# Bias tables of a two-block transformer: one matmul for a table's heads, and a DMA that repeats its eight rows

## Chip, cores and metric

One NeuronCore of a Trainium2 chip. The metric is device time in microseconds, the median of several executions; all times of this document are of that one core.

## The reference

Two transformer blocks on 512 tokens of width 1024, all in fp32. Every layer is `x + norm(mixer(norm(x)))`, then `x + norm(ffn(norm(x)))`. What the change touches are two bias tables that are added to attention scores:

```python
# block 1, dilated attention: 3 groups of 8 heads, dilations 1, 4, 16, bands of 128
bucket = t5_bucket(np.clip(m, 0, band) * dilation)          # m = i + band - k
bias = jnp.transpose(bias_table[bucket], (2, 0, 1))         # bias_table: 32 buckets x 8 heads
logits = einsum('bxhnqd,bxhnkd->bxhnqk', qs, kk) * scale + bias
logits = jnp.where(mask, logits, NEG_INF)
...
# block 2, differential attention: 4 heads of two maps, rel_bias_2 of 32 buckets x 8
bias = rel_bias[t5_bucket_2(k_pos[None, :] - q_pos[:, None])]
```

The bias depends on the difference of two positions alone, so a head's bias is a Toeplitz matrix: one row of values, shifted by one from each query to the next.

## The kernel before

The order of work is: block 1 (dilated attention, an FFN with a convolution, a linear recurrence, a second such FFN), then block 2 (three mixers side by side, attention over a memory, an FFN with squared ReLU; twice). Activations stand feature-major in SBUF (`hT`) as a high and a low part of reduced fp32, and every weight product is three matmuls: L161 (high, high), L162 (high, low), L163 (low, high), 512 columns each. A block of 128 outputs is 8 × 3 = 24 of them. A weight comes as a raw tile of 512 KB from HBM by SP's queue (L141, three raw buffers); ScalarE casts the high part (L148), VectorE subtracts for the low part (L149); five such pairs can be held. All DMAs of this document are issued by SP, in the order of its instructions, and an instruction that waits holds up those behind it.

The Python code is generators that run side by side; a Tile framework then sets the order of the instructions on each engine from the emission order, priorities and the buffers of the pools. So a step that is emitted earlier, or costs less, can move others.

A bias table is made by `toeplitz` (L275 to 288). `oh` is a constant one-hot matrix of 33 rows (32 buckets and a mask row) by L columns, `tb` the bias table of buckets by heads. For a head the matmul L285 takes `oh` as the moving operand and the head's column of `tb`, repeated to 128 columns, as the stationary one, so that the head's row of L values stands on all 128 output partitions. fp32 matmuls appear as two records each. ScalarE copies them (L286) to a staging tile `fz` of 128 × 1024, and when that is full a DMA (L288) writes it to a DRAM scratch of [128 rows, heads, L]. Reading the scratch with a row pitch one less than a row gives the shifted rows (`toeplitz_view`), for `bias` (L403 to 405, tile `bi`) in block 1 and for `da` (L1057, tile `bd`) in block 2.

There are four tables: tz0 (L = 383), tz1 and tz2 (L = 255) in `setup` of `attn` (L311 to 324), and `da_scr` (L = 639, 32 rows) in `setup2` (L791). The staging tile of tz0 is one of the four buffers of tag "qk"; that of the others is the single buffer of tag "scr", which is also the scratch of the norms' squares (`rms`, L199).

What sets when the tables are made: `START` (L83) is the list of steps before the first products, in which each `t0` is one head of tz0; the rest follow between the first Q and K blocks. `setup2` and what follows it in `prep` (the keys and values of the memory, `mem_kv`, and small columns) are `fill` of the second FFN of block 1: after each block of its up products (`ups`) from the eighth on, one `next(fill)` runs one step; a head of the table is a step.

Of the kernel before, what the change touches and what calls it, by code (L numbers as in the profile page):

```python
# [31 lines left out]
def pipe(gens):  # L32
    """software pipeline: each round starts one generator (None: no new one) and advances the ones under way"""
    live = []
    for g in gens:
        if g is not None:
            live.append(g)
        live = [x for x in live if next(x, 0) is None]
        yield
    while live:  # L40
        live = [x for x in live if next(x, 0) is None]
        yield
# [11 lines left out]
def both(*gens):  # L54
    """generators run side by side, as one; a step that ends with "more" goes on after the others' steps"""
    live = list(gens)
    while live:
        r = [next(g, 0) for g in live]
        while "more" in r:
            r = [next(g, 0) if v == "more" else v for g, v in zip(live, r)]  # L60
        live = [g for g, v in zip(live, r) if v is None]
        yield


def woven(*streams):
    """streams of (generator, steps per round), until all end"""
    live = list(streams)
    while live:
        live = [(g, n) for g, n in live if all([next(g, 0) is None for _ in range(n)])]
        yield  # L70
# [11 lines left out]
# order of the first norms (n: a step of a tile's), weights (w) and heads of the bias table (t)  # L82
START = "n0 t0 t0 t0 n0 n1 n0 w0 w1 n1 n2 n2 n1 n3 n2 n3 n3".split()  # L83
# mixers of the second block: units of attention by tile and head (d: differential, s: stick-breaking pair,
# m: latent pair), the projections emitted beside them (c, v: by tile; l: weights; u: latent up-projection by tile;
# s: stick-breaking by block), and how many output products follow each further round
# [6 lines left out]
class Net:  # L93
# [31 lines left out]
    def bank(self):  # L125
        """accumulator bank"""
        return self.ps.tile([P, 512], F32, tag="acc", name=self.nm("acc"), bufs=6)

    def tbank(self):
        """bank for transposes"""  # L130
        return self.ps.tile([P, 512], F32, tag="tr", name=self.nm("tr"), bufs=2)

# [1 line left out]
    def weight(self, src, shape, pool=None, tag="w", lo=None):  # L134
        """src: HBM view of shape [128, a, b] with a*b <= 1024, split into hi + lo."""
        return self.cut(self.load(src, shape), shape, pool, tag, lo)
# [15 lines left out]
    def w_in(self, W, c0, width=P):  # L152
        """feature-major weight blocks: [128 k, 8 kb, width]"""
        return self.weight(W[:, c0:c0 + width].rearrange("(k p) c -> p k c", p=P), (W.shape[0] // P, width))
# [10 lines left out]
    def split_to(self, dst, src, hi=None):  # L165
        """dst [P, 2, ...] hi/lo of src (fp32 view in SBUF or PSUM)"""
        self.nc.scalar.copy(dst[:, 0], src)  # L167
        self.nc.vector.tensor_sub(dst[:, 1], src, dst[:, 0].bitcast(F32))  # L168

# [6 lines left out]
    def rsqrt(self, ss, scale, shape, tag):  # L176
        """rsqrt(ss * scale + EPS) on a small fp32 tile"""
# [15 lines left out]
    def rms(self, hs, n=D):  # L193
        """1/rms over the free axis of the two halves hs"""
# [10 lines left out]
    def to_T(self, src, dst, t):  # L205
        """src [P tok, 1024] -> dst[:, hi/lo, kb, t*128..]"""
# [9 lines left out]
    def prenorm(self, t, gb, dst=None, src=None, xn=None):  # L216
        """steps: the row's rms, the normalised tile (scaled by ScalarE where VectorE is the busier), its transposes"""
# [16 lines left out]
    def postnorm(self, hs, y, t, gb):  # L234
        """x[t] += rmsnorm(hs) * g, by way of y"""
# [7 lines left out]
    def after(self, t, xn=None):  # L243
        """x[t] is final for this sublayer: start the next sublayer's norm, or store"""
        if self.next_g is None:
            self.nc.sync.dma_start(self.out[t * P:(t + 1) * P], self.x[:, t])
            return
        if self.next_gb is None:
            self.next_gb = self.bcast_row(self.next_g)
        yield from self.prenorm(t, self.next_gb, xn=xn)  # L250

    # feature-major block: psum[128 cols, 512 tok] over all 8 kb
# [7 lines left out]
    def cols(self, srcs, n, pool, name):  # L260
        """each src (n*128 values, contiguous in HBM) -> tile [128, len(srcs), n], value n*128+p at [p, n]"""
# [13 lines left out]
    def toeplitz(self, table, oh, L, heads, scratch, stage, bank=None):  # L275
        """rows F[h, t] = sum_b table[b, h] * oh[b, t], repeated on 128 rows of HBM scratch [128, heads, L]"""
        nc = self.nc
        kb = oh.shape[0]
        per = 1024 // L
        for h0, h1 in halves(heads, per):  # L280
            f = stage()
            for h in range(h0, h1):
                for c0, c1 in halves(L, 512):
                    b = (bank or self.tbank)()
                    nc.tensor.matmul(b[:, :c1 - c0], table(h).to_broadcast([kb, P]), oh[:, c0:c1], start=True, stop=True)  # L285
                    nc.scalar.copy(f[:, (h - h0) * L + c0:(h - h0) * L + c1], b[:, :c1 - c0])  # L286
                yield
            nc.sync.dma_start(scratch[:, h0:h1], f[:, :(h1 - h0) * L].rearrange("p (h t) -> p h t", t=L))  # L288

    def toeplitz_view(self, scratch, L, h0, nh, c0, n):  # L290
        """[128 i, nh, n]: F[h, c0 + kk - i]"""
# [3 lines left out]
    def attn(self, l):  # L295
# [4 lines left out]
        with ExitStack() as cx:  # L300
# [10 lines left out]
            def setup():  # L311
                tb = one.tile([33, 24], F32, name="tb")
                nc.sync.dma_start(tb[:32], a["rel_bias"])
                nc.vector.memset(tb[32:33], NEG)
                for g in range(3):
# [5 lines left out]
                    yield from self.toeplitz(lambda h, g=g: tb[:, g * 8 + h:g * 8 + h + 1], oh, LS[g], 8, scr[g],  # L321
# [52 lines left out]
            def start():  # L374
                """norms of the four tiles and the first values' weights, in the order of their use"""
# [241 lines left out]
    def exp_small(self, out, x, pool, n):  # L617
        """exp on a small [128, n] fp32 tile, x in [-87, 88] after clamping"""
# [20 lines left out]
    def log_sigmoid(self, x, out, pool, n):  # L639
        """out = min(x, 0) - log1p(exp(-|x|)) on a small [128, n] tile"""  # L640
# [18 lines left out]
    def lru_setup(self, one):  # L659
        """per-channel constants of the recurrent mixer"""  # L660
# [117 lines left out]
    def out_proj(self, W, A, yt, gpost, mid):  # L778
        """yt[t] = (8 k-blocks A) @ W, then x += rmsnorm(yt) * gpost; mid(g) emits g, the first half of K, and
        returns a pool for weights of the second one"""  # L780
# [12 lines left out]
    def setup2(self, pool):  # L793
        """bias rows of the differential attention, masks, rope tables"""
# [3 lines left out]
        tb = pool.tile([32, 8], F32, name="tb2")  # L798
        nc.sync.dma_start(tb, a["rel_bias_2"])
        oh = self.nrm.tile([P, D], F32, tag="xn", name=self.nm("oh"))[:32, :L]  # L800
        nc.sync.dma_start(oh, a["c_ohda"])
        yield from self.toeplitz(lambda h: tb[:, h:h + 1], oh, L, 8, self.da_scr,
# [7 lines left out]
    def prep(self, l, pool):  # L810
        """what layer l of the second block needs beside its tokens"""
# [45 lines left out]
    def head_rstd(self, src, nh, dh, tag):  # L857
        """1/rms per head of src [P, nh, dh]"""
# [7 lines left out]
    def proj_tok(self, W, c0, width, consume, early=False):  # L866
        """token-major h @ W[:, c0:c0+width]: one generator per token tile, then consume(t, bank)"""
# [19 lines left out]
    def below(self, x, fill=0.0):  # L887
        """fills a [128, 128] block on and above its diagonal"""
# [3 lines left out]
    def exp_rows(self, p, stat, w):  # L892
        """p = exp(p - max), stat [P, 2]: max in, sum out"""
# [4 lines left out]
    def trans_blocks(self, src, n, pool):  # L898
        """transposes of n 128-column blocks of src [P, n*128] -> tile [P, n*128]"""
# [8 lines left out]
    def o_scaled(self, b, nh, dh, c, pool, tag, bufs):  # L908
        """rmsnorm over each head of b * c (c [P, nh] or None) -> token-major tile"""
# [16 lines left out]
    def y_write(self, on, nb, gcol, kb, i):  # L926
        """transposes on [P tok, nb*128], scales by gcol per feature, hi/lo into hT[:, :, kb:kb+nb, tile i]"""
# [10 lines left out]
    def mem_kv(self, l):  # L938
        """keys and values of the memory, a generator"""
# [33 lines left out]
    def mix(self, l):  # L973
        a, nc = self.a, self.nc
        W, Wo = a["w_in_2"][l], a["w_out_2"][l]
        with ExitStack() as cx:
# [64 lines left out]
            # one attention unit = one head (pair) of one query tile  # L1041
# [244 lines left out]
            def gate(*what):  # L1286
                """until all of what is done"""
# [3 lines left out]
            def settle():  # L1291
                """the layer's input back, and the memory attention's buffers"""
# [28 lines left out]
            def paced(g, ns):  # L1321
                """g, by ns steps per round, then by one"""
# [13 lines left out]
    def memory(self, l, x2, b_qz, b_o, b_n, b_g, ons):  # L1336
        """memory attention of one token tile, in buffers of 1024 columns"""
# [82 lines left out]
    def ff_head(self, l):  # L1420
        """first blocks of ffn2(l) for the tokens of the last two tiles, while the first tile is still on its way"""
# [68 lines left out]
    def down_gen(self, W, ks, A, tail):  # L1490
        """token-major partial product over k-blocks ks; tail(t, half, bank) consumes each."""
# [15 lines left out]
    def down_last(self, W, ks, A, tail, post=None, pool=None):  # L1507
        """as down, one token tile after another, each followed by post(t) and the next sublayer's norm"""
# [131 lines left out]
```

## Time and profile before

| | us |
|---|---|
| three executions | 3063.64, 3059.31, 3063.38 |
| median | 3063.38 |
| the profiled execution, its span | 3061.5 |
| TensorE busy in it | 3012.3 |
| VectorE, ScalarE, GpSimd busy | 1669.2, 1254.2, 170.5 |

The profile is of one execution, taken on the chip. Its span is the time from the first instruction's start to the last one's end. A timeline lists one engine's instructions by start time; in brackets stands how long the engine had been idle before one and what ended that. `out<-in` names the tiles by the program's names, and `x4` is four instructions in a row. Engines are PE (TensorE), DVE (VectorE), ACT (ScalarE), POOL (GpSimd), SP; SPq rows are DMA issues.

### The profile page before, as it was taken

How to read it: one execution, taken by the hardware profiler on the slowest of the kernel's cores; microseconds unless marked ns; L12 is line 12 of the kernel's file. 1: busy time of each engine (PE TensorE's matmuls, PEld its weight loads, DVE VectorE, ACT ScalarE, POOL GpSimd, SP SyncE). 2: the span in 40 equal slices, each digit the busy share in tenths (PEclk: the TensorE clock that was granted, in tenths of full speed). 3: DMA queues.
4: the chain of work that ended last, by engine and by line, in shares of the span. 5: the costliest groups of instructions: out<-in, count | busy, mean ns of one | idle time of the engine just before them, and what ended most of it. 6: DMA issues, size and time to landing. Idle time of an engine off the chain costs nothing.

```text
span 3061.5 us, 37833 instructions
## 1 busy us (share of the span) xinstructions
PE 3012.3 (98%) x14594; PEld 2488.2 (81%) x14594; DVE 1669.2 (55%) x3166; ACT 1254.2 (41%) x2427; POOL 170.5 (6%) x257
## 2 busy tenths in 40 slices
PE   9999999999999999999999999999999999999999
PEld 6889898888888877877787777888887877888887
DVE  3232323364655696644557678754545578754443
ACT  4232322354333575433335467542323457632222
POOL 0000000000000041000001022000000013000000
PEclk9999999999999999999999999999999999999999
DMA  6221222333333323333334332132333333123332
GB/s 185 71 83 56 83 63 76 97 102 92 97 96 91 89 75 112 100 98 107 105 97 138 103 118 84 28 124 84 118 94 111 110 86 104 49 76 91 96 95 70
DMA packets 340023, 287.40 MB, mean 94 GB/s; under 512 B 14041, under 2 KB 280676, under 8 KB 339844
## 3 DMA queue, kind: packets, MB, share of 16 engines
q1 hardware_dynamic: 339844, 284.99, 30.7%
q8 instruction: 115, 1.88, 0.3%
q14 instruction: 64, 0.52, 0.1%
HBM read 272.34 MB, written 12.62 MB: 93 GB/s over the span
## 4 chain that ended last, share of the span: by engine, by line
PE 54%; DVE 6%; ACT 2%; issue 1%; POOL 1%; DMA 1%; POOLq 0%; ACTq 0%; DVEq 0%
PE acc L161 16%; PE acc L163 16%; PE acc L162 16%; PE acc L1048 1%; PE tr L212 1%; PE acc L1061 1%; PE tr L903 1%; DVE w L149 1%; PE acc L1193 1%; PE acc L1387 0%; PE acc L1367 0%; DVE z L1105 0%; DMA raw<-in_w_in_dram 0%; ACT w L148 0%; PE tr L285 0%
## 5 line engine op out<-in xcount | busy, mean ns | idle before, releaser
L149 DVE TENSOR_TENSOR w<-raw,w 128x1024 fp32r<-128x1024 f32 (+1 forms) x456 | 553.9, 1217 | 489.2 <-ACT w L148 488.6
L161 PE MATMUL acc<-hT,w 128*128 128x512 f32 (+1 forms) x1992 | 761.0, 383 | 1.5 <-ACT w L148 1.2
L163 PE MATMUL acc<-hT,w 128*128 128x512 f32 (+1 forms) x1992 | 757.6, 380 | 3.0 <-DVE w L149 2.8
L162 PE MATMUL acc<-hT,w 128*128 128x512 f32 (+1 forms) x1992 | 759.0, 381 | 0.4 <-DVE hT L168 0.4
L148 ACT CAST w<-raw 128x1024 fp32r<-128x1024 f32 (+2 forms) x464 | 477.9, 1033 | 551.5 <-PE acc L163 469.3
L163 PEld LDWEIGHTS acc<-hT,w 128*128 128x128 f32 x1992 | 374.9, 188 | 83.5 <-DVE w L149 4.3
L161 PEld LDWEIGHTS acc<-hT,w 128*128 128x128 f32 x1992 | 374.4, 188 | 82.9 <-issue 2.6
L162 PEld LDWEIGHTS acc<-hT,w 128*128 128x128 f32 x1992 | 374.6, 188 | 78.5 <-DVE hT L168 1.1
L161 PE MATMUL acc<-w,act 128*128 128x512 f32 x896 | 355.1, 397 | 0.8 <-ACT act L167 0.8
L162 PE MATMUL acc<-w,act 128*128 128x512 f32 x896 | 354.3, 396 | 0.0
L163 PE MATMUL acc<-w,act 128*128 128x512 f32 x896 | 352.8, 394 | 0.0
L161 PE MATMUL acc<-w,hT 128*128 128x256 f32 (+2 forms) x896 | 335.1, 374 | 0.8 <-ACT w L148 0.8
L163 PE MATMUL acc<-w,hT 128*128 128x256 f32 (+2 forms) x896 | 326.0, 364 | 0.0
L162 PE MATMUL acc<-w,hT 128*128 128x256 f32 (+2 forms) x896 | 325.1, 363 | 0.0
L562 DVE SCALAR_TENSOR_TENSOR u<-acc,cw,u 128x511 f32<-128x511 f32 x192 | 143.5, 748 | 205.9 <-ACT u L560 202.8
L161 PEld LDWEIGHTS acc<-w,hT 128*128 128x128 f32 x896 | 205.6, 229 | 21.1 <-issue 2.4
L162 PEld LDWEIGHTS acc<-w,hT 128*128 128x128 f32 x896 | 205.8, 230 | 17.1 <-issue 2.4
L163 PEld LDWEIGHTS acc<-w,hT 128*128 128x128 f32 x896 | 205.6, 229 | 15.2
L161 PEld LDWEIGHTS acc<-w,act 128*128 128x128 f32 x896 | 168.3, 188 | 42.6 <-ACT act L167 2.1
L163 PEld LDWEIGHTS acc<-w,act 128*128 128x128 f32 x896 | 168.3, 188 | 41.3 <-DVE act L168 0.6
L162 PEld LDWEIGHTS acc<-w,act 128*128 128x128 f32 x896 | 168.4, 188 | 39.2
L560 ACT ACTIVATE u<-acc,cw 128x512 f32<-128x512 f32 x96 | 74.7, 778 | 219.5 <-PE acc L163 219.3
(376 smaller groups left out, 3307.5 us busy)
## 6 DMA issues: line engine op xcount, KB each, us to landing
raw<-in_w_ff_dram SPq DMA_DIRECT2D x128, 512.0 KB
raw<-in_ffn_w_up_dram SPq DMA_DIRECT2D x96, 512.0 KB
raw<-in_attn_w_qkv_dram SPq DMA_DIRECT2D x72, 512.0 KB
raw<-in_ffn_w_down_dram SPq DMA_DIRECT2D x48, 512.0 KB
raw<-in_w_in_dram SPq DMA_DIRECT2D x40, 512.0 KB
raw<-in_lru_w_in_dram SPq DMA_DIRECT2D x16, 512.0 KB
raw<-in_w_out_dram SPq DMA_DIRECT2D x16, 512.0 KB
x<-in_x_dram SPq DMA_DIRECT2D x8, 512.0 KB
```

Source lines behind the costliest of these rows:

```text
L148: nc.scalar.copy(w[:, 0], raw)
L149: (lo or nc.vector).tensor_sub(w[:, 1], raw, w[:, 0].bitcast(F32))
L161: mm(out, sh, mh, start=first, stop=False)
L162: mm(out, sh, ml, start=False, stop=False)
L163: mm(out, sl, mh, start=False, stop=last)
L212: nc.tensor.transpose(b[:, j * P:(j + 1) * P], src[:, k * P:(k + 1) * P], self.ident)
L560: nc.scalar.activation(u, b, AF.Identity, bias=cw[:, 3, j:j + 1], scale=cw[:, 2, j:j + 1])
L562: nc.vector.scalar_tensor_tensor(u[:, s:], b[:, :S - s], cw[:, i, j:j + 1], u[:, s:], op0=ALU.mult, op1=ALU.add)
L903: nc.tensor.transpose(b[:, j * P:(j + 1) * P], src[:, j * P:(j + 1) * P], self.ident)
L1048: nc.tensor.matmul(o[:, oc:oc + dv], pT[:, k * P:(k + 1) * P], v(k), start=(k == 0), stop=(k == i))
L1061: nc.tensor.matmul(b[:, :w], QZ[:, h, m, i * P:(i + 1) * P], kT[:, h, :w], start=True, stop=True)
L1193: nc.tensor.matmul(b[:, :w], MT[:96, i, 0, h], MT[:96, :i + 1, 1, h], start=True, stop=True)
```

## The change

One matmul makes a whole table: the stationary operand is a slice of 128 columns of `tb`, of which the first eight are the heads of the table, so head h's row stands on output partition h alone (the other partitions hold other columns or zeros and are not copied). One copy takes eight partitions, and one DMA per table reads the eight rows, each 128 times (a step of 0 in the source), and writes the same scratch. `tb` becomes 33 × 144, `tb2` 32 × 128, the added columns zeroed on VectorE. A table is one step of the generator. Nothing that reads the scratch is changed; comments and docstrings were taken out of the file as well, so line numbers move by two to four.

```diff
-START = "n0 t0 t0 t0 n0 n1 n0 w0 w1 n1 n2 n2 n1 n3 n2 n3 n3".split()
+START = "n0 t0 n0 n1 n0 w0 w1 n1 n2 n2 n1 n3 n2 n3 n3".split()
...
     def toeplitz(self, table, oh, L, heads, scratch, stage, bank=None):
         nc = self.nc
-        kb = oh.shape[0]
-        per = 1024 // L
-        for h0, h1 in halves(heads, per):
-            f = stage()
-            for h in range(h0, h1):
-                for c0, c1 in halves(L, 512):
-                    b = (bank or self.tbank)()
-                    nc.tensor.matmul(b[:, :c1 - c0], table(h).to_broadcast([kb, P]), oh[:, c0:c1], start=True, stop=True)
-                    nc.scalar.copy(f[:, (h - h0) * L + c0:(h - h0) * L + c1], b[:, :c1 - c0])
-                yield
-            nc.sync.dma_start(scratch[:, h0:h1], f[:, :(h1 - h0) * L].rearrange("p (h t) -> p h t", t=L))
+        f = stage()
+        for c0, c1 in halves(L, 512):
+            b = (bank or self.tbank)()
+            nc.tensor.matmul(b[:, :c1 - c0], table, oh[:, c0:c1], start=True, stop=True)
+            nc.scalar.copy(f[:heads, c0:c1], b[:heads, :c1 - c0])
+        nc.sync.dma_start(scratch.rearrange("r h t -> h r t"), f[:heads, None, :L].to_broadcast([heads, P, L]))
+        yield
...
             def setup():
-                tb = one.tile([33, 24], F32, name="tb")
-                nc.sync.dma_start(tb[:32], a["rel_bias"])
-                nc.vector.memset(tb[32:33], NEG)
+                tb = one.tile([33, 16 + P], F32, name="tb")
+                nc.vector.memset(tb[:, 24:], 0.0)
+                nc.sync.dma_start(tb[:32, :24], a["rel_bias"])
+                nc.vector.memset(tb[32:33, :24], NEG)
...
-                    yield from self.toeplitz(lambda h, g=g: tb[:, g * 8 + h:g * 8 + h + 1], oh, LS[g], 8, scr[g],
+                    yield from self.toeplitz(tb[:, g * 8:g * 8 + P], oh, LS[g], 8, scr[g],
...
     def setup2(self, pool):
-        tb = pool.tile([32, 8], F32, name="tb2")
-        nc.sync.dma_start(tb, a["rel_bias_2"])
+        tb = pool.tile([32, P], F32, name="tb2")
+        nc.vector.memset(tb[:, 8:], 0.0)
+        nc.sync.dma_start(tb[:, :8], a["rel_bias_2"])
...
-        yield from self.toeplitz(lambda h: tb[:, h:h + 1], oh, L, 8, self.da_scr,
+        yield from self.toeplitz(tb, oh, L, 8, self.da_scr,
```

SP's queue at the start, before (the names are tiles; `tz_132` is tz0's scratch, `raw` a weight, `oh` a one-hot matrix of the 255-column tables):

```order
L288 DMA tz_132<-fz_133 128x766
L288 DMA tz_132<-fz_141 128x766
L141 DMA raw_347<-in_attn_w_qkv_dram 128x8x128
L141 DMA raw_381<-in_attn_w_qkv_dram 128x8x128
L141 DMA raw_417<-in_attn_w_qkv_dram 128x8x128
L317 DMA oh_481<-in_c_oh_dram 33x255
L317 DMA oh_513<-in_c_oh_dram 33x255
L141 DMA raw_451<-in_attn_w_qkv_dram 128x8x128
```

And the same place of SP's queue in the changed kernel, with the semaphores that each row waits for (DMAHW is a DMA's landing; `tz_133`, `tz_283` and `tz_341` are tz0, tz1 and tz2):

```order
L284 DMA tz_133<-fz_134 8x128x383 [waits DMAHW1_49,Activation_49]
L315 DMA oh_281<-in_c_oh_dram 33x255 [waits DMAHW2_49,DVE_49,PE_49]
L315 DMA oh_339<-in_c_oh_dram 33x255 [waits DMAHW3_49,DVE_49,PE_49]
L141 DMA raw_349<-in_attn_w_qkv_dram 128x8x128 [waits DMAHW4_49]
L403 DMA bi_378<-tz_133 128x2x256 [waits DMAHW5_49,DMAHW1_49]
L141 DMA raw_384<-in_attn_w_qkv_dram 128x8x128 [waits DMAHW6_49,Activation_49]
L284 DMA tz_283<-fz_284 8x128x255 [waits DMAHW7_49,Activation_49]
L141 DMA raw_415<-in_attn_w_qkv_dram 128x8x128 [waits DMAHW0_49]
L141 DMA raw_446<-in_attn_w_qkv_dram 128x8x128 [waits DMAHW4_49,DVE_49]
L284 DMA tz_341<-fz_342 8x128x255 [waits DMAHW2_49,Activation_49]
```

The first Q and K weights (raw_347, raw_381 before, raw_349, raw_384 now) moved from the place right behind the first transfers of tz0 to behind the two `oh` loads, the second of them also behind a read of tz0; and tz1 and tz2 moved up between them.

ScalarE at the first Q blocks, before (`q` is the evacuation of a Q block, `w` a weight's cast):

```order
L148 CAST w_419<-raw_417 128x1024 [waits DMAHW5_49]
L148 CAST w_453<-raw_451 128x1024 [waits DMAHW0_49,DVE_49,PE_49]
L370 COPY x<-acc_291 128x512 [waits PE_49]
L286 COPY fz_341<-acc_342 128x383 [waits PE_49]
L148 CAST w_553<-raw_551 128x1024 [waits DMAHW1_49,DVE_49]
L336 ACTIVATE q_236<-acc_346 128x512 [waits PE_49]
L148 CAST w_620<-raw_618 128x1024 [waits DMAHW2_49,DVE_49,Activation_49]
```

And there in the changed kernel:

```order
L368 COPY x<-acc_290 128x512 [waits DVE_49,PE_49]
L283 COPY fz_284<-tr_285 8x255 [waits PE_49,Activation_49]
L148 CAST w_351<-raw_349 128x1024 [waits DMAHW4_49]
L148 CAST w_386<-raw_384 128x1024 [waits DMAHW6_49]
L334 ACTIVATE q_230<-acc_348 128x512 [waits PE_49]
L334 ACTIVATE q_230<-acc_383 128x512 [waits PE_49]
L283 COPY fz_342<-tr_343 8x255 [waits DMAHW7_49,Activation_49]
L148 CAST w_417<-raw_415 128x1024 [waits DMAHW0_49]
```

Before, five weights are cast ahead of the first evacuation; now two are, and the third stands behind the copy of tz2, which waits for the landing of tz1.

ScalarE before the norm of the memory in block 1's second FFN, before:

```order
L286 COPY fz_10501<-tr_10502 128x512
L286 COPY fz_10501<-tr_10505 128x127
L148 CAST w_10692<-raw_10690 128x1024
L167 CAST act_10497<-u_10487 128x512
L199 ACTIVATE sq_10595,ss_10596<-mem_10591 128x512 x2
L199 ACTIVATE sq_10680,ss_10681<-mem_10676 128x512 x2
```

And now, with the waits:

```order
L283 COPY fz_9599<-tr_9600 8x512 [waits PE_49]
L283 COPY fz_9599<-tr_9603 8x127 [waits PE_49]
L167 CAST act_9590<-u_9580 128x512 [waits DVE_49]
L558 ACTIVATE u_9667<-acc_9607,cw 128x512 [waits PE_49]
L148 CAST w_9800<-raw_9798 128x1024 [waits DMAHW1_49]
L566 ACTIVATE u_9667<-u_9667 128x512 [waits DVE_49,Activation_49]
L558 ACTIVATE u_9672<-acc_9608,cw 128x512 [waits PE_49]
L167 CAST act_9677<-u_9667 128x512 [waits DVE_49]
L199 ACTIVATE sq_9693,ss_9694<-mem_9689 128x512 [waits DMAHW5_49,DMAHW2_49,Pool_49]
L199 ACTIVATE sq_9693,ss_9694<-mem_9689 128x512
L148 CAST w_9835<-raw_9833 128x1024 [waits DMAHW3_49]
```

The square (`sq`) stood behind the last of eight copies before and stands behind the only one now; the casts of the next up block (w_9835) stand behind it. On TensorE 144 weight products lie between the table's two matmuls and the transposes of this norm in the changed kernel (over 210 between the last table matmuls and these transposes before). The place of the transposes (`tr_9989<-ident,xn_9692`; `acc_9768` is the last of the down products ahead, `acc_9831` the next up block) is now

```order
L161 MATMUL acc_9768<-w_9800,act_9590 128x512
L162 MATMUL acc_9768<-w_9800,act_9590 128x512
L163 MATMUL acc_9768<-w_9800,act_9590 128x512
L212 MATMUL tr_9989<-ident,xn_9692 128x128
L161 MATMUL acc_9831<-hT,w_9835 128x512
L162 MATMUL acc_9831<-hT,w_9835 128x512
L212 MATMUL tr_9989<-ident,xn_9692 128x128 x3
```

so the next up block comes behind the first of these transposes, which comes behind the norm.

## Rows read from the trace of the kernel before

**Rows 1.** The page's head: the span, and each engine's busy time, share of the span, instructions.

```profile
span 3061.5 us, 37833 instructions
PE 3012.3 (98%) x14594; PEld 2488.2 (81%) x14594; DVE 1669.2 (55%) x3166; ACT 1254.2 (41%) x2427; POOL 170.5 (6%) x257
```

**Rows 2.** TensorE's timeline from the start: start, duration, line, out<-in; what ended idle time.

```profile
3.08 4.17 PE L285 MATMUL acc<-oh,tb 33*128 33x383 f32 x6 [3.08 <-DMA oh<-in_c_oh_dram]
9.04 1.97 PE L212 MATMUL tr<-ident,xn 128*128 128x128 f32 x8 [1.80 <-DVE xn L229]
12.29 1.64 PE L285 MATMUL acc<-oh,tb 33*128 33x383 f32 x2
```

**Rows 3.** TensorE's timeline around one head of table 0, between two Q blocks.

```profile
30.71 0.50 PE L161 MATMUL acc<-hT,w 128*128 128x512 f32 x1
36.17 0.40 PE L163 MATMUL acc<-hT,w 128*128 128x512 f32 x1
36.50 0.91 PE L285 MATMUL acc<-oh,tb 33*128 33x383 f32 x2
37.34 0.50 PE L161 MATMUL acc<-hT,w 128*128 128x512 f32 x1
```

**Rows 4.** TensorE's timeline around two heads of table 1, and the first scores.

```profile
56.08 0.40 PE L163 MATMUL acc<-hT,w 128*128 128x512 f32 x1
56.40 1.12 PE L285 MATMUL tr<-oh,tb 33*128 33x255 f32 x4
57.46 0.50 PE L161 MATMUL acc<-hT,w 128*128 128x512 f32 x1
68.03 3.30 PE L428 MATMUL acc<-k,q 128*128 128x128 f32 x16
```

**Rows 5.** TensorE's timeline around one head of block 2's table.

```profile
1349.56 0.40 PE L163 MATMUL acc<-hT,w 128*128 128x512 f32 x1
1349.89 1.34 PE L285 MATMUL tr<-oh,tb 32*128 32x512 f32 x4
1351.16 0.50 PE L161 MATMUL acc<-hT,w 128*128 128x512 f32 x1
```

**Rows 6.** Line L288, the table DMAs: who waited for them (us, times).

```profile
  ACT fz L286: 5.8, 3
  ACT sq L199: 0.4, 1
```

**Rows 7.** The page's costliest groups: the low and the high part of a weight.

```profile
L149 DVE TENSOR_TENSOR w<-raw,w 128x1024 fp32r<-128x1024 f32 (+1 forms) x456 | 553.9, 1217 | 489.2 <-ACT w L148 488.6
L148 ACT CAST w<-raw 128x1024 fp32r<-128x1024 f32 (+2 forms) x464 | 477.9, 1033 | 551.5 <-PE acc L163 469.3
```

**Rows 8.** The DMA view: the table transfers, their count and KB each.

```profile
da_scr<-fz SPq DMA_DIRECT2D x8, 319.5 KB
tz<-fz SPq DMA_DIRECT2D x4, 510.0 KB
tz<-fz SPq DMA_DIRECT2D x4, 383.0 KB
```

**Rows 9.** Two windows: busy PE, PEld, DVE, ACT, POOL; PEclk, DMA share, GB/s.

```profile
10.00:20.00 10.00, 9.23 (x45) 7.54 (x44) 7.68 (x12) 7.28 (x17) 1.10 (x2) 1.00 0.94 301
1163.00:1173.00 10.00, 7.11 (x19) 5.38 (x20) 9.39 (x12) 5.15 (x7) 0.00 (x0) 0.66 0.43 118
```

**Rows 10.** SP's timeline: the first Q and K weights.

```profile
14.85 2.72 SPq L141 DMA_DIRECT2D raw<-in_attn_w_qkv_dram  x3
```

**Rows 11.** ScalarE's timeline: the first norm's squares.

```profile
5.91 0.63 ACT L199 ACTIVATE sq<-x 128x512 f32<-128x512 f32 x1 [0.71 <-DMA x<-in_x_dram]
```

**Rows 12.** TensorE's timeline after a stall of 2.84 us in a later stage.

```profile
1166.62 0.80 PE L163 MATMUL acc<-hT,w 128*128 128x512 f32 x1 [2.84 <-DVE w L149]
1167.22 0.63 PE L161 MATMUL acc<-hT,w 128*128 128x512 f32 x1
1171.85 0.39 PE L163 MATMUL acc<-hT,w 128*128 128x512 f32 x1
```

## The prediction, made before the changed kernel ran

> **What bounds the kernel now.** I read the page's head first: TensorE is busy 3012.3 of 3061.5 us [rows 1], so some 49 us of the whole span are not its own work, and whatever takes TensorE work away shortens the kernel unless TensorE then waits for something else. Next I read TensorE's timeline around each table. The reader is to see the table matmuls standing in the middle of the stream of weight products, with nothing idle beside them [rows 2 to 5]. Then I read who waits for the table transfers: ScalarE, 5.8 us in three waits for a staging buffer, and 0.4 us before the memory norm [rows 6]. So in the kernel before, the transfers cost nothing on TensorE and the table matmuls cost their full length.
>
> **What is removed, by duration.**
> Table 0 (383 columns). The first three heads take 4.17 us from 3.08, and TensorE stands before its next work until 9.04 anyway [rows 2]: their removal is worth nothing. The fourth costs 1.64 [rows 2]. Heads five to eight each sit between two weight products: from the product before to the product after it is 37.34 − 36.17 = 1.17, and products otherwise follow each other every (36.17 − 30.71) / 23 = 0.24, so one costs 0.93 and four cost 3.7 [rows 3].
> Tables 1 and 2 (255 columns): a pair costs 57.46 − 56.08 − 0.24 = 1.14, so 0.57 a head [rows 4]; 14 of 16 go, 8.0 us. Six of these heads stand behind the first scores (68.03), 3.4 us of the 8.0.
> Block 2 (639 columns): 1351.16 − 1349.56 − 0.24 = 1.36 a head [rows 5]; seven go, 9.5 us.
> Sum of the gain on TensorE: 1.6 + 3.7 + 8.0 + 9.5 = 22.8 us.
> ScalarE loses 35 copies. It waits for others in all these stretches, so this is worth nothing by itself. The two added memsets stand at places where VectorE has no work of the path (the first while the first loads are on their way); at most they are one VectorE operation of the costly kind, 1.22 us [rows 7]; I take 0.
>
> **What is added: the same bytes out of eight partitions.** Before, each table left 128 partitions in transfers of 128 rows: 4 × 383 KB for table 0 (tz0), 2 × 510 KB each for tables 1 and 2 (tz1, tz2), 8 × 319.5 KB for block 2 [rows 8]; at 1024 bytes to a KB that is 1.57, 1.04, 1.04 and 2.62 MB. Now each is one transfer from 8 partitions. No row shows a transfer that reads so few partitions, so I bound its rate. In the busiest stretch the sixteen engines move 301 GB/s at a share of 0.94 [rows 9], 320 at full share. Upper end: the transfer has eight outer rows, so it may use as few as half of the engines, each at its full rate, 160 GB/s. Lower end: the rate goes with partitions, 320 × 8 / 128 = 20 GB/s. The ends are a factor of eight apart and the nearest row (128 partitions, sixteen engines) decides only the upper one, so I take the geometric middle, 57 GB/s, and keep both.
> [...]
>
> **What waits at the start (57 GB/s).** Two things move. On SP's queue the first Q and K weights, issued from 14.85 on right behind the first tables [rows 10], now stand behind the 255-column tables' oh loads, which wait for TensorE's transposes of the last norms; tz1 stands behind a bias load that waits for tz0's landing, and tz2 behind third and fourth weight blocks. On ScalarE the casts that ran two blocks ahead now stand behind the copy into fz, which waits for the table before it. And a weight of 128 rows uses the engines that the table occupies, so it lands when the table has.
> - The queues are at 0.94 until some 12 us with x tiles and weights. tz0: 12 + 1569/57 (27.5) = 39.5. First Q weight behind it; cast 1.03 and low part 1.22 [rows 7] with their semaphores, some 3.5: first Q product at 43 (before: 30.71 [rows 3]). Two blocks of 5.7 end at 54.
> - tz1 is issued about 43, 1044/57 = 18.3 us: 62. Copy, cast, low part: third block at 66; TensorE stands 11 us. Two blocks end at 77.
> - tz2 issued at 66 lands at 85; fifth block at 88.5, another 11 us idle; it ends at 94.5. First scores at 94.5 in place of 68.03 [rows 4]: **+26.5**, the removed work before them already counted.
> - The removed heads behind them: **−3.4**.
>
> **What waits in block 2.** The copy of the table is issued at once, 2617/57 = 46 us. The square of the memory norm (ScalarE, sq) uses the same one buffer as fz. Before, its wait was 0.4 us, since the last small copy was a transfer of 319.5 KB [rows 6, 8]. Now it waits the 46 us, about 1 after the matmul. From sq to the transposes takes 9.04 − 5.91 = 3.1 us in the first norm [rows 2, 11]. So the transposes start 50 us after the table matmul. In the changed order they stand 144 weight products behind it, 144 × 0.24 = 34 us (the shifts of the other fillers move nothing that waits). ScalarE's casts stand behind sq too, so TensorE idles 50 − 34 = **+16**, and the gain there is **−9.5**.
> **The clock.** [...] At the start a loss ahead of a landing is absorbed by it; two remain, the last stall there and that in block 2: **+4.8**.
> Everything later moves unchanged: the small columns and the memory keys come some steps earlier and hide behind products as before, 0.
> **Sum:** 26.5 − 3.4 + 16 − 9.5 + 4.8 = +34.4 on 3061.5. The profiled execution's own span stands 1.9 below the median, so I add to the median: 3063.4 + 34.4 = 3097.8, say **3098**.
>
> **Rivals.**
> *Hidden transfers, faster.* The eight engines run at full rate, 160 GB/s, or the rows are spread over all sixteen, so that the eight partitions are no limit. tz0 lands at 22, tz1 takes 6.5 us and the block-2 table 16, well inside the 34. What is left of the waits: the first, third and fifth Q blocks still find a cast some 2 us late, since the casts lost their lead (6), and the memory norm's transposes wait some 3.5 for a square now close ahead of them. −22.8 + 9.5 = −13.3: 3050. It decides from where the landings stop mattering. At 80 GB/s: tz0 lands at 31.6, first block 35, tz1 48, third block 51.5, tz2 51.5 + 13 = 64.5, fifth 68, scores 74 (+6); −3.4; block 2: 33 + 4 − 34 = 3, −9.5; clock and slips 4: 0. So **above some 80 GB/s it is faster, below slower**. For it: the bytes do not grow and the upper bound comes from a row. Against: no row shows a source of few partitions.
> [...]
> *Near the crossing, the same.* Between 77 and 84 GB/s the two cancel: 3063, a narrow case.
> *Strictly by partition.* 20 GB/s: tz0 78 us, tz1 and tz2 52 each: scores at 12 + 78 + 3.5 + 52 + 3.5 + 52 + 3.5 + 6 = 210 (+142), −3.4; block 2: 131 + 4 − 34 = 101, −9.5; clock 5: +235, 3298.
> *Not the saving it says.* Were TensorE to take eight times as long for the eight-row output, 22.8 us would stay. One matmul has the form of one head before (33 or 32 rows in, 128 columns of stationary), so this is excluded by the rows.
>
> **How the numbers follow.** A measurement of this kernel tells 0.2% (6 us) from no change. Forecast, slower by the table transfers, 0.70; hidden transfers 0.23; the same 0.05; by partition 0.02. The forecast's own range, from 72 GB/s (+11: tz0 is 5.7 shorter, tz1 and tz2 3.8 each, block 2 9.6) to 48 (+55, the same four terms longer by 5.2, 3.5, 3.5 and 8.6), is 3075 to 3119. The range takes in the faster rival and a little below: 3047 to 3120.
>
> **What would show it.** In the changed profile: an empty TensorE of some 11 us before the first, the third and the fifth Q block, each ended by a weight cast whose raw waited behind a table; the first scores at about 94; ScalarE's sq before the memory norm waiting tens of us for da_scr; table transfers of 27, 18, 18 and 46 us. Transfers of 10, 7, 7 and 16 us and first scores near 65 would make the prediction wrong.

## The result, and the profile after

| | us |
|---|---|
| kernel before, median of 4 | 3062.62 |
| changed kernel, median of 4 (3103.58 to 3105.08) | 3104.45 |
| ratio, 95% interval | 1.014 [1.0126, 1.0155] |
| span of the profiled execution, before and after | 3061.5, 3101.8 |

It is slower by some 42 us; 3098 had been predicted. Every kernel of this document was timed with the kernel before run beside it, whose median was 3060.85 to 3062.62. The page's head of the changed kernel (compare [rows 1]):

```profile
span 3101.8 us, 37640 instructions
PE 2989.4 (96%) x14524; PEld 2481.5 (80%) x14524; DVE 1671.6 (54%) x3168; ACT 1242.0 (40%) x2392; POOL 170.5 (5%) x257
```

TensorE has 22.9 us less work (3012.3 to 2989.4), and the span is 40.3 longer, so 63.2 us of idle time were added. Where they lie is read by cutting both spans at the same five events: the first scores, the first product with the values, the last scores, the first matmul of block 2's table, the first scores of block 2. The windows of the kernel before (columns as in [rows 9]):

```profile
0.00:68.03 68.03, 62.39 (x284) 46.52 (x284) 25.78 (x34) 30.83 (x58) 3.01 (x13) 1.00 0.61 184
68.03:212.40 144.37, 143.97 (x687) 126.13 (x686) 43.49 (x131) 43.71 (x107) 0.00 (x0) 1.00 0.29 86
212.40:586.70 374.30, 373.42 (x1882) 336.98 (x1883) 108.12 (x281) 96.94 (x208) 0.00 (x0) 1.00 0.24 71
586.70:1349.50 762.80, 747.51 (x3542) 611.47 (x3541) 479.52 (x677) 354.50 (x532) 59.01 (x58) 0.99 0.32 95
1349.50:1744.20 394.70, 391.89 (x1704) 309.53 (x1704) 225.95 (x344) 155.27 (x242) 18.20 (x20) 1.00 0.36 110
1744.20:3061.50 1317.30, 1293.14 (x6502) 1057.58 (x6500) 786.33 (x1703) 572.98 (x1283) 90.23 (x166) 1.00 0.30 91
```

and of the changed kernel:

```profile
0.00:104.28 104.28, 57.36 (x254) 45.26 (x255) 25.09 (x34) 25.00 (x43) 3.02 (x13) 0.82 0.61 124
104.28:244.40 140.12, 139.76 (x675) 124.24 (x673) 44.65 (x133) 42.81 (x101) 0.00 (x0) 1.00 0.29 86
244.40:618.60 374.20, 373.37 (x1883) 337.09 (x1884) 108.23 (x281) 97.11 (x208) 0.00 (x0) 1.00 0.24 71
618.60:1379.60 761.00, 747.44 (x3544) 611.25 (x3543) 480.31 (x677) 354.90 (x534) 58.19 (x58) 1.00 0.32 96
1379.60:1786.30 406.70, 380.64 (x1673) 306.13 (x1672) 226.98 (x344) 149.46 (x227) 17.96 (x20) 0.97 0.38 105
1786.30:3101.80 1315.50, 1290.85 (x6502) 1057.51 (x6500) 786.39 (x1703) 572.77 (x1283) 91.36 (x166) 1.00 0.29 91
```

First column after the colon: the length. From window to window the change is **+36.3, −4.3, −0.1, −1.8, +12.0, −1.8**, in all +40.3 (the two −1.8 are within the spread of the kernel before, 3059.3 to 3063.6). Two stages lose: the start, and the stage with block 2's table. Who TensorE waited for in the changed kernel (us in total, times, longest):

```profile
PE tr L212 <- DVE xn L229: 32.7, 8, 24.7
PE acc L161 <- ACT w L148: 23.1, 3, 11.4
PE tr L282 <- DMA oh<-in_c_oh_dram: 14.2, 1, 14.2
```

The 24.7 is the wait before the memory norm's transposes; the other two are the start, as TensorE's timeline shows (answers to [rows 3, 4]; the number in brackets is the idle time ahead):

```profile
44.26 2.04 PE L282 MATMUL tr<-oh,tb 33*128 33x255 f32 x4 [14.15 <-DMA oh<-in_c_oh_dram]
46.91 0.80 PE L161 MATMUL acc<-hT,w 128*128 128x512 f32 x1 [0.61 <-ACT w L148]
72.47 0.79 PE L161 MATMUL acc<-hT,w 128*128 128x512 f32 x1 [11.38 <-ACT w L148]
96.96 0.79 PE L161 MATMUL acc<-hT,w 128*128 128x512 f32 x1 [11.06 <-ACT w L148]
```

Now the transfers. SP's timeline, with ScalarE's next to it, gives issue and landing of each table; a landing is read from the first instruction that stood waiting for it (answers to [rows 8, 10]; `...` stands for rows left out):

```profile
5.69 0.37 SPq L284 DMA_DIRECT2D tz<-fz  x1
21.35 4.82 SPq L315 DMA_DIRECT2D oh<-in_c_oh_dram  x2
43.83 0.39 SPq L403 DMA_DIRECT2D bi<-tz  x1
45.92 0.30 SPq L284 DMA_DIRECT2D tz<-fz  x1
...
70.06 0.30 SPq L284 DMA_DIRECT2D tz<-fz  x1
...
93.64 0.36 SPq L403 DMA_DIRECT2D bi<-tz  x1
...
1381.14 0.30 SPq L284 DMA_DIRECT2D da_scr<-fz  x1
```

```profile
69.67 0.36 ACT L283 COPY fz<-tr 8x255 f32<-8x255 f32 x1 [7.94 <-DMA tz<-fz]
71.38 1.04 ACT L148 CAST w<-raw 128x1024 fp32r<-128x1024 f32 x1 [1.34 <-DMA raw<-in_attn_w_qkv_dram]
...
95.87 1.04 ACT L148 CAST w<-raw 128x1024 fp32r<-128x1024 f32 x1 [21.69 <-DMA raw<-in_attn_w_qkv_dram]
...
1435.37 0.63 ACT L199 ACTIVATE sq<-mem 128x512 f32<-128x512 f32 x1 [40.20 <-DMA da_scr<-fz]
```

tz0 is issued at 5.69, and the bias load that waits for it goes out at 43.83: 38.1 us for 1.57 MB, 41 GB/s. tz1: 45.92 to the copy into its buffer at 69.67, 23.8 us, 44 GB/s. tz2: 70.06 to 93.64, 23.6 us, 44 GB/s. Block 2: 1381.14 to ScalarE's square at 1435.37, 54.2 us for 2.62 MB, 48 GB/s. The square waited 40.2 us, where it had waited 0.4 before [rows 6]. Over this last transfer the sixteen DMA engines are busy half of the time and move little, other traffic included (columns as in [rows 9]):

```profile
1381.00:1435.00 54.00, 32.80 (x141) 26.07 (x139) 13.58 (x19) 4.48 (x7) 0.00 (x0) 0.84 0.50 59
```

A share of 0.50 at 59 GB/s, where a share of 0.94 went with 301 [rows 9]: the engines that are busy are slow, which a limit by the number of engines alone does not give.

### The profile page after: what moved, and what is told of

Same layout as the page of the kernel before. It is cut to its first block, busy times and chain, and to the rows that moved or that the text cites. A ratio compares the mean times of both kernels' runs of the same rounds, so it can differ in the third digit from the quotient of the medians.

```text
span 3101.8 us, 37640 instructions
## 1 busy us (share of the span) xinstructions
PE 2989.4 (96%) x14524; PEld 2481.5 (80%) x14524; DVE 1671.6 (54%) x3168; ACT 1242.0 (40%) x2392; POOL 170.5 (5%) x257
## 5 line engine op out<-in xcount | busy, mean ns | idle before, releaser
L202 POOL TENSOR_TENSOR ss<-ss,mhalf 128x1 f32<-128x1 f32 x60 | 44.4, 741 | 2035.9 <-DVE ss L201 2035.8
```

Source lines behind the costliest of these rows:

```text
L202: nc.gpsimd.tensor_tensor(ss[:, 3:4], ss[:, 2:3], self.mhalf[:, :1], op=ALU.pow)
```

## The experiments

Two questions were open. Is it the eight neighbouring partitions of the source that make a table slow, or the eight engines? And who holds up TensorE: the shared staging buffer, or the weights queued behind the transfer?

**The eight rows spread out (e_ports).** The columns of `tb` are placed so that head h comes out on partition 12h; beside that one VectorE copy for each `tb` is added and the copies on ScalarE take 96 partitions.

```diff
-            nc.scalar.copy(f[:heads, c0:c1], b[:heads, :c1 - c0])
-        nc.sync.dma_start(scratch.rearrange("r h t -> h r t"), f[:heads, None, :L].to_broadcast([heads, P, L]))
+            nc.scalar.copy(f[:96, c0:c1], b[:96, :c1 - c0])
+        nc.sync.dma_start(scratch.rearrange("r h t -> h r t"), f[:96:12, None, :L].to_broadcast([heads, P, L]))
...
+                nc.vector.tensor_copy(tw[:, :96].rearrange("b (h s) -> b s h", s=12)[:, :3], tb.rearrange("b (g h) -> b g h", g=3))
```

> The eight rows stand on partitions 0, 12, ... 84 in place of 0 to 7; same matmuls, same eight-row transfers, same order of SP's queue. If the side of the memory that the eight neighbouring partitions share sets the rate (the theory), the eight rows now leave by eight ways: tables at 130 GB/s or more, da_scr lands within 20 us of its issue, the idle times of 14, 11, 11 and 25 us are gone but for 1 to 3 us each, and the time is 3048 to 3060 us. If eight engines are the limit, or a rate per partition (the rivals), nothing changes: 41 to 48 GB/s and 3100 to 3108 us.

Measured 3046.45 us, ratio 0.9951 [0.9936, 0.9965]: 15.6 us faster than before, 58 faster than the change, and 1.6 below the lower end of what was expected. SP's issue and ScalarE's square that waits for the landing, of this kernel:

```profile
1346.37 0.70 SPq L284 DMA_DIRECT2D da_scr<-fz  x1
```

```profile
1362.11 0.63 ACT L199 ACTIVATE sq<-mem 128x512 f32<-128x512 f32 x1 [1.73 <-DMA da_scr<-fz]
```

15.7 us in place of 54.2: 166 GB/s, from the same number of partitions by the same number of rows. So neither eight engines nor a rate per partition set the 41 to 48 GB/s; where the eight partitions lie did. 166 is close to the upper end of the prediction, half of sixteen engines' 320; whether the eight engines or the places of the rows set the 166 is not separated here.

**How the gap decides (e_step2, e_step16).** The same with rows on partitions 0, 2, ... 14 and 0, 16, ... 112 (the slices, and the placing of the columns to fit).

> The eight rows stand on partitions 0, 2, ... 14. [...] If only a row's own partition counted, it would be as slow as the changed kernel; if any gap between rows were enough, as fast as with a gap of 12.

> The eight rows stand on partitions 0, 16, ... 112, farther apart than with the gap of 12 that gave 171 GB/s. [...] If distance alone counted (the rival), it would be as fast as with a gap of 12: 160 to 175 GB/s, da_scr in 15 to 17 us, 3045 to 3048 us.

Measured 3049.36 us, ratio 0.9958 [0.9942, 0.9975], and 3050.5, ratio 0.996 [0.9945, 0.9974], the second 2.5 above what distance alone would have given. (The 171 GB/s of the second expectation is the gap of 12, for which the two rows above give 166.) Issue and landing of block 2's table, first of e_step2:

```profile
1348.61 0.70 SPq L284 DMA_DIRECT2D da_scr<-fz  x1
```

```profile
1377.43 0.63 ACT L199 ACTIVATE sq<-mem 128x512 f32<-128x512 f32 x1 [14.78 <-DMA da_scr<-fz]
```

and of e_step16:

```profile
1345.82 0.63 SPq L284 DMA_DIRECT2D da_scr<-fz  x1
```

```profile
1374.56 0.63 ACT L199 ACTIVATE sq<-mem 128x512 f32<-128x512 f32 x1 [14.73 <-DMA da_scr<-fz]
```

28.8 and 28.7 us: 91 GB/s both, neither as slow as the changed kernel nor as fast as the gap of 12, though one lies within 15 partitions and the other over 113. Distance is not it, nor is any gap enough. The landing takes 54.2, 28.8 or 28.7, and 15.7 us, so it nearly halves twice. The four layouts show that the places decide; what in the places decides is not shown.

**All 128 partitions, still one matmul (e_rep).** The stationary operand holds the eight heads sixteen times, so output partition p holds head p mod 8; one DMA reads 128 partitions, each row eight times.

```diff
+        st = oh[:, 768:768 + P]
+        nc.vector.tensor_copy(st.rearrange("b (r h) -> b r h", h=heads), table[:, None, :heads].to_broadcast([oh.shape[0], P // heads, heads]))
...
-            nc.tensor.matmul(b[:, :c1 - c0], table, oh[:, c0:c1], start=True, stop=True)
-            nc.scalar.copy(f[:heads, c0:c1], b[:heads, :c1 - c0])
-        nc.sync.dma_start(scratch.rearrange("r h t -> h r t"), f[:heads, None, :L].to_broadcast([heads, P, L]))
+            nc.tensor.matmul(b[:, :c1 - c0], st, oh[:, c0:c1], start=True, stop=True)
+            nc.scalar.copy(f[:, c0:c1], b[:, :c1 - c0])
+        nc.sync.dma_start(hbm(scratch, 0, [[L, P], [P * L, heads], [1, L]]), f[:, None, :L].to_broadcast([P, heads, L]))
```

> Still one matmul per table, but its stationary operand holds the eight heads sixteen times, so that all 128 output partitions are used, and one DMA per table reads 128 partitions, each row eight times. Every theory of the source expects the old rate of sixteen engines (250 to 320 GB/s, da_scr in 8 to 12 us): 3044 to 3056 us, that is the 22.8 us of table matmuls less some 6 to 10 us of weights that are still late at the start. If the time stays at 3100, the bytes or the number of packets would be the cause, not the source.

Measured **3033.83 us, ratio 0.991 [0.9894, 0.9927]**: the best version of this study, 28 us faster than before and 71 faster than the change. The 13 us after its issue of block 2's table, as a window (columns as in [rows 9]), and TensorE's longest waits in the whole run:

```profile
1337.00:1350.00 13.00, 13.00 (x57) 10.49 (x56) 6.88 (x11) 5.67 (x11) 0.02 (x1) 1.00 0.88 282
```

```profile
PE tr L212 <- DVE xn L229: 7.5, 7, 3.6
PE acc L163 <- POOL w L149: 6.2, 2, 3.9
PE acc L284 <- DMA oh<-in_c_oh_dram: 3.2, 1, 3.2
```

282 GB/s at a DMA share of 0.88, the weights behind the table included, and none of the waits above is left. It is 10 us below the expectation: no weight is late at the start, where 6 to 10 us had been allowed for, and block 2 gains more than its term (the next experiment). The first scores come at 60.08.

**Only block 1 changed, twice (e_b1, e_rep_b1).** Block 2's table goes back to `toeplitz` as it was before, once in the changed kernel, once in e_rep (`toeplitz_old` is that function as it was).

```diff
-        yield from self.toeplitz(tb, oh, L, 8, self.da_scr,
+        yield from self.toeplitz_old(lambda h: tb[:, h:h + 1], oh, L, 8, self.da_scr,
```

> Only block 1's tables are made the new way; block 2's as before, eight matmuls and eight transfers from 128 partitions. The stage of block 2's table took 12 us longer in the changed kernel than before, so by the stage table 3090 to 3095 us, with first scores still at 104 and no idle time before the memory norm's transposes. If block 2's loss were an after-effect of the start, it would stay at 3104.

> The version that read 128 partitions (3033.8 us, 28 below before) with block 2's table made as in the kernel before. If each table is worth its matmuls, block 1 alone is worth 13.3 us of the prediction's terms: 3047 to 3051 us, and block 2 the rest, 15 us, 5 more than its 9.5. If the surplus of 5 us comes from the start, it is 3042 to 3046.

e_b1: 3092.53 us, ratio 1.0098 [1.0083, 1.0113], 11.9 below the change: the stage table's 12.0. The start's waits are unchanged and the 24.7 is gone from TensorE's waits:

```profile
PE acc L161 <- ACT w L148: 22.3, 3, 10.9
PE tr L282 <- DMA oh<-in_c_oh_dram: 13.8, 1, 13.8
PE tr L212 <- DVE xn L229: 7.6, 8, 3.7
```

e_rep_b1: 3047.99, ratio 0.9954 [0.994, 0.9968]. Block 1 by itself is worth 12.9 us, where its terms of the sum made 13.3; block 2 is worth the 14.2 between the two medians (15.3 if each is taken against its own runs of the kernel before), where its term was 9.5. TensorE's work differs by 13.3 us between the two kernels (2993.9 and 2980.6), of which the table's own matmuls are 9.4. The surplus lies behind the table's first matmul: from there to the first matmul of L1192 (L1207 in e_rep_b1) e_rep_b1 takes 535.3 us and e_rep 521.4, 13.9 more, 2.3 of it idle time. A head also delays the second product behind it: in e_rep_b1 the product before the first head starts at 1335.01 and the second one behind it at 1336.94, 1.93 apart, where two spacings are 0.47. That is 1.46 a head in place of 1.36, 10.2 for seven. The last 1.4 stay open.

**The staging buffer apart (e_own).** Block 2's staging tile comes from the tile of a mask that is filled later, so the square of the memory norm has its buffer to itself. For room `tb` and `oh` share one tile, and the mask is filled behind `mem_kv`; neither is printed here.

```diff
...
-                                 lambda: self.nrm.tile([P, D], F32, tag="scr", name=self.nm("fz"), bufs=1))
-        self.cmask = pool.tile([P, 512], F32, name="cmask")
-        nc.gpsimd.memset(self.cmask, 0.0)
...
+        self.cm = pool.tile([P, 640], F32, name="cmask")
+        yield from self.toeplitz(tb, oh, L, 8, self.da_scr, lambda: self.cm)
+        self.cmask = self.cm[:, :512]
```

> Block 2's staging tile is taken from another buffer (that of a mask, which is filled later), so that the square of the memory norm no longer waits for the transfer; the transfer itself is as slow as in the changed kernel. If the shared buffer alone made the 24.7 us of idle TensorE (the theory of the prediction), they go: 3077 to 3082 us. If the weights queued behind the transfer on its eight engines land only with it (the rival), some 20 us of idle time stay, now ended by a weight's cast: 3095 to 3105 us.

Measured 3098.21 us, ratio 1.012 [1.0105, 1.0135], 6.2 below the change. The square now runs at 1360.07, before the table is even made, and yet TensorE stands; TensorE's and ScalarE's timelines there:

```profile
1440.19 0.80 PE L161 MATMUL acc<-hT,w 128*128 128x512 f32 x1 [17.84 <-ACT w L148]
```

```profile
1439.09 1.04 ACT L148 CAST w<-raw 128x1024 fp32r<-128x1024 f32 x1 [14.51 <-DMA raw<-in_ffn_w_up_dram]
```

Of the 24.7 us 17.8 are left, and they end with a cast whose weight, an ordinary transfer from HBM, stands behind the table in SP's queue. Its landing fits the table's own: issued at 1383.22, the table would land at 1437.4 if it took the 54.2 us of the changed kernel, an estimate, since nothing in this kernel waits for it early. SP's timeline:

```profile
1383.22 0.31 SPq L284 DMA_DIRECT2D da_scr<-cmask  x1
1384.36 18.54 SPq L141 DMA_DIRECT2D raw<-in_ffn_w_up_dram  x1
1402.99 26.36 SPq L949 DMA_DIRECT2D mem<-in_mem_dram  x1
```

TensorE goes on 57.0 us after the table's issue (1440.19), and in the changed kernel 57.4 (1438.52, after 1381.14). So freeing the buffer did not end the wait earlier: TensorE ran some 6.5 us more of products before it stood, and the 6.2 us gained are that. The weights alone hold TensorE until about the table's landing, as the rival had it; what freeing the weights alone would give was not run. The rows show one thing more: behind the table SP itself stands in its next two issues, 18.5 and 26.4 us, where a weight's issue takes 0.37 in the median of the changed kernel and the table's own took 0.31.

**Another queue (e_actq).** The tables are issued by ScalarE (`nc.scalar.dma_start`), so that nothing stands behind them on SP.

> The four table transfers are issued by ScalarE in place of SP, so SP's weights no longer stand behind their waits, and the weights are in another queue. If an engine serves its queues in turn, weights land within a few us while a table goes on, the three idle times before Q blocks shrink to under 5 us each and the bias loads alone wait for tables: 3065 to 3085 us. If the table holds up whatever comes to the same eight engines, whichever queue it comes by, it stays at 3095 to 3108 us.

Measured 3114.52 us, ratio 1.0172 [1.0157, 1.0187]: 10 us worse than the change, and outside both ranges. At the start no weight stands behind a table in SP's queue, but tz0, now issued by ScalarE at 5.29, holds up the first Q weight, which SP issues at 5.40 with no instruction ahead of it that waits for a table. SP's timeline, and ScalarE's cast of that weight:

```profile
5.40 0.63 SPq L141 DMA_DIRECT2D raw<-in_attn_w_qkv_dram  x1
```
```profile
38.76 1.04 ACT L148 CAST w<-raw 128x1024 fp32r<-128x1024 f32 x1 [17.15 <-DMA raw<-in_attn_w_qkv_dram]
```

The weight lands 33 us after its issue; the bias load that waits for tz0 goes out at 40.73, 2 us behind this cast. The fourth norm's square stands behind the cast. TensorE's longest waits are now 33.7 us at block 2's table and 16.6 before the last norm's transposes:

```profile
PE acc L161 <- DVE yacc L598: 34.0, 2, 33.7
PE tr L212 <- DVE xn L229: 24.8, 10, 16.6
```

So at the start the other queue did not carry the weight past the table. The 33.7 us are another matter: there ScalarE's square waits 43.3 us for the shared buffer with two weight casts behind it, and TensorE starts (1437.95) as the first of them ends. The order on ScalarE and SP moved too in this kernel, so its time isn't a measure of the queue alone.

## Why the prediction was right, and where its steps were off

The sign, its cause and the size held: 3098 against 3104.45, inside the forecast's own range of 3075 to 3119. That it came so close is in part luck. With the transfers as measured (10.6, 5.5 and 5.3 us longer at the start, 8.2 in block 2) its own sum would be some 3127; other terms, given below, erred the other way. By its steps:

- **The work removed.** TensorE's work fell by 22.9 us where the sum had 22.8 on the path. The two don't count the same: 2.6 us of the heads at the very start were work but not on the path, and slow products after stalls add work (0.79 to 0.80 us for the first behind a stall, 0.39 to 0.40 at full clock). In the kernel without these stalls (e_rep) 28.2 us were gained, so the 22.8 was some 5 low, all of it in block 2, whose 9.5 measured 14.2 to 15.3.
- **The rate.** 57 GB/s was a middle between two bounds; measured 41 to 48. No row stood behind the middle itself, so its nearness is luck. The upper bound (160) turned out to be what the same transfer does when its rows are spread (166).
- **The start.** +26.5 was predicted, +36.3 measured: first scores at 104.3. The mis-sized term is the three transfers: 38.1, 23.8 and 23.6 us in place of 27.5, 18.3 and 18.3, with tz0 starting at 5.7 and not after the queues are free at 12, and with tz1 and tz2 issued 2.1 and 0.4 us after the landing before them, where the sum had some 4. The three idle times stand where they were expected, 14.8, 11.4 and 11.1 against "some 11". The first of them was ended by something else than a weight's cast: by a one-hot load of 33 rows, queued behind tz0, on which the next table's matmul waits, and TensorE's first Q product stands behind that matmul. The second and third were ended by the cast as predicted.
- **After the scores.** −3.4 predicted, −4.3 measured.
- **Block 2.** +16 for the wait and −9.5: +6.5, with 2.4 for the clock +8.9; measured +12.0. The wait was 24.7 instead of 16; 8 of the 8.7 more come from the transfer (54 for 46). The work saved was more too, 14.2 for 9.5. The step that named the cause was half right: the square did wait 40.2 us for the shared buffer, but with the buffer apart 17.8 us stay, since the weights land no earlier. The prediction had written that of the start ("it lands when the table has") and not carried it to block 2.
- **The clock.** The granted clock is low in the stretches that hold a stall, here from 44 to 72 and around the 24.7 us:

```profile
44.00:72.00 28.00, 16.18 (x52) 11.70 (x52) 2.45 (x2) 4.54 (x7) 0.00 (x0) 0.74 0.60 108
1416.00:1440.00 24.00, 1.49 (x5) 1.22 (x6) 2.60 (x4) 3.42 (x6) 0.55 (x1) 0.54 0.48 71
```

  Behind the second and third stall it is 0.50 from 72.4 to 76 and from 97 to 100; after the 24.7 us it is back at 1.00 from 1444 on. The first products last 0.80 us as in [rows 12]. Behind the first stall 48 products start within 13.8 us (46.91 to 60.70) where at full clock they would within 11.0 (47 × 0.233, the spacing of the products from 200.00 to 204.89, where the granted clock is 1.00), behind the second within 13.0 (72.47 to 85.51), and behind the third 24 within 7.2 (96.96 to 104.12) in place of 5.4. That is 2.8, 2.1 and 1.8 us, a little of it a wait for the low part of a weight. The sum's +4.8 takes 2.4 for each of two stalls, an estimate of the author's that no run shows; the three at the start, 2.2 in the mean, are what was measured in its place, and for block 2 it was not taken apart.
- **The rival of hidden transfers** ended at 3050; e_ports, which is that rival made true, ran at 3046.45. The crossing lies between 48 GB/s (+41.8 us) and 91 (−12.4, the mean of the two kernels there); a straight line in landing time, 54.2 and 28.8 us, puts it at 35 us, 76 GB/s, an estimate, where 80 was predicted.

## What to carry to other kernels

When a DMA reads SBUF, look at which partitions its rows stand on before counting bytes: the same 2.62 MB took 54, 29 or 16 us from eight partitions, by their places alone. If one matmul can make the rows, it can as well make them on 128 partitions, by repeating the stationary columns, at no cost on TensorE (busy 2980.6 us in e_rep, 2989.4 in the changed kernel). And a slow transfer need not be alone: here weights issued behind it or by another queue landed about when it did, so that freeing the buffer gained 6 of 25 us and changing the issuing engine none.

## What was not expected

- With the transfers out of the way block 2's table was worth 14.2 us, and its matmuls account for 9.4 of it.
- The kernel's time hardly tells the 28.8 us transfer from the 15.7 one (3049.4 and 3050.5 against 3046.5), since TensorE has products to cover either: in e_step2 the norm's transposes come 35.1 us after the issue, with 2.4 us idle before them.
- Behind a slow table SP's own next issues took up to 26.4 us.
- Issuing from ScalarE made the kernel 10 us slower than issuing from SP.
- SP's issue of block 2's table with a gap between rows takes 0.63 to 0.70 us, against 0.30 for rows on partitions 0 to 7; no wait on TensorE is put down to it.
